# Hybrid backbone step: another order of the mixer's projections, conv's end amid attention, and other halves of the output projection

## Chip, cores and metric

The kernel runs on one core of one Trainium2 chip, in float32 throughout. The metric is device time in microseconds of one execution; lower is better. The kernel before takes 2477.6 us, the median of 3 runs (2476.86 to 2482.67).

## The reference, cut to what matters

Two layers work on 512 latent and 128 context tokens (640 columns in all) of width 1024. Each layer is a half-step FFN, a mixer, and a second half-step FFN. The change touches the mixer alone:

```python
h = _rms(x, norm_g[1]) * (1.0 + sc2) + sh2
u = h @ w_in                                        # 1024 -> 1536 columns
o_pool = _pool_mixer(u[..., :256], pool_w, pool_scale)   # 4 groups: mean over 2/4/8/16 minus token, 64x64 map, scale
glu = u[..., 256:512] * sigmoid(u[..., 512:768])         # conv: value * sigmoid(gate)
y = depthwise_conv(glu, 31 taps, centred) + b
o_conv = silu(_rms(y, conv_norm_g)) @ conv_pw            # 256 -> 256
q, k, v = ...                                       # 8 query heads, 2 key/value heads of 64, RMS norm on q and k
o_attn = context attention, or latent attention (band of +-128 plus 128 cached keys, 2-D rotary), with a sink per head
x = x + g2 * (concat([o_pool, o_conv, o_attn]) @ w_out)  # 256 + 256 + 512 -> 1024
```

## The kernel before, in words

Channels lie on the 128 partitions and tokens along the free axis. Every float32 product is made from three products of a high and a low part (`h*h`, `h*l`, `l*h`), each on 320 of the 640 columns. A chunk of the input projection is 128 output channels: 8 blocks of input channels, 3 parts, 2 halves of the tokens, 48 products in `product`, line 379. `u_chunks` yields two such chunks for a load of 256 columns (1 MB). ScalarE writes the high part of the weights (line 358), VectorE the low part (line 359).

The function is written as generators, and a scheduler puts each engine's instructions in a fixed order from the order in which they are written, a priority, and its own reckoning of time. Engines take their queues in that order and wait on each other by semaphores. `tc.high_priority(offset=AHEAD)` puts an attention batch 200 instructions ahead of where it is written.

`mixer` goes through these pieces. `ORDER` ahead of attention: conv's gate `cg`, keys and values `kv`, the first two query chunks `q0`, conv's value `ca`. Keys take three steps (`k_steps`): their norm, their transposes and caches, and the rotary embedding with the split into high and low part. Queries pass through `query_heads`: square, norm (a chain of small VectorE operations on 128x10), rotary multiplications on POOL, and the split. `BEHIND`, woven into attention: the other query chunks `q1`, pooling `pl` (two chunks and two small products `po`), and the first half of the output projection (`out_chunks`, eight chunks of 24 products).

Attention has four channel pairs `c` of two heads, and each has two batches of blocks, (0, 1) and (2, 3, 4); after a batch there are two or three steps, 20 in all, numbered `i`. A batch makes scores (line 1080, two PSUM banks), takes the maximum on VectorE (line 1083), the exponential and a scaling on ScalarE (1091, 1095), transposes through one bank on TensorE (1098) with copies back on ScalarE (1099), the value products (1105, one bank), and the split into `mixa` (826, 827). At step `i` the loop pops `FILL[i]` modulation steps for later sub-layers, runs taps, conv's steps and `PLAN[i]` background steps.

Conv's 31 taps per channel chunk are `conv_taps`. Chunk 0's taps, and the first and the last four of chunk 1, run on VectorE (lines 928 and 930). The other 26 of chunk 1 are a scaled copy on ScalarE (933) into one scratch buffer `cm` and an addition on POOL (934). `TAP_PLAN` gives the taps of each step. At `i == CONV_AT`, 15 here, the rest of the taps is written and `convolution` begins; it has six steps, one at each `i` from there: sum of squares, norm (323 to 329), its spread (335, 336), a swish of each chunk (1035 to 1044), and two product chunks `cp` with their splits. The last step comes after the loop.

The second half of the output projection is `into_ffn`, line 743: it works half the tokens after the other and goes over into the second FFN. Before, part 0 takes blocks 0, 1, 4, 5 of the concatenated input (pool, and attention's first two pairs), part 1 takes 6, 7, 2, 3 (attention's last two, then conv).

Scratch buffers of 640 or more columns come from one pool of seven (`tmp`), larger ones from one of six (`act`), weights as loaded from one of two (`raw`). The mixer's scaled input `xa` lies in the phase's own pool until its end.

Of the kernel before, what the change touches and what calls it, by code (L numbers as in the profile page):

```python
# [16 lines left out]
P = 128  # L17
D = 1024
KD = D // P
# [32 lines left out]
CONV_AT = 15  # L52
TAP_PLAN = ((3, 2, 1, 2, 3, 2, 0, 2, 2, 1, 3, 2, 0, 2, 1, 3, 1, 1, 1, 3), (2, 4, 3, 3, 4, 4, 4, 2, 0, 4, 1, 1, 0, 1, 2, 1, 2, 0, 1, 4))
ORDER, BEHIND = ("cg", "kv", "q0", "ca"), ("q1", "pl")
PLAN = (0, 1, 0, 1, 0, 2, 0, 1, 0, 0, 0, 1, 1, 1, 2, 1, 1, 1, 1, 0)
# [43 lines left out]
def backbone(ctx: ExitStack, tc: tile.TileContext, ins, consts, y_prompt, y_sample, out_k, out_v):  # L99
# [8 lines left out]
    def phase(name):  # L108

        if "cm" in scope:  # L110
            scope.pop("cm").__exit__(None, None, None)
        cm = tc.tile_pool(name=name, bufs=1, reuse_waits="tile")
        scope["cm"], scope["pool"] = cm, cm.__enter__()

# [268 lines left out]
    def new_xa(name):  # L383
        return tuple(scope["pool"].tile([P, KD, T + 2], F32R, tag="xa", name=f"{name}_{t}", bufs=2) for t in "hl")
# [399 lines left out]
    def mixer(l, xa, R, tab, fill):  # L784
# [179 lines left out]
        def pooling():  # L964
# [39 lines left out]
            catch_up()  # L1004
            for c, (ph, pl) in enumerate(parts):
                w = (pw[0][:, c:c + 1, :], pw[1][:, c:c + 1, :])
                pa, pb = product(w, lambda k: (ph, pl), 1, 0, f"po{l}{c}")
                m = act([P, 2, T], F32R, f"mixp{l}{c}")
# [6 lines left out]


        def convolution():
# [9 lines left out]
            RC = rstd_spread(dg, tmp(f"RC{l}"), bank_pair(f"rc{l}"))  # L1027
# [3 lines left out]
            for c in range(2):  # L1031
# [7 lines left out]
                th = tmp(f"cth{l}{c}")  # L1039
                A.activation(out=th, in_=z, func=AF.Tanh, scale=hg)  # L1040
                V.scalar_tensor_tensor(out=z, in0=th, scalar=1.0, in1=z, op0=ALU.add, op1=ALU.mult)
                hh, hl = tmp(f"ch{l}{c}", dt=F32R), tmp(f"cl{l}{c}", dt=F32R)
# [4 lines left out]
            for c in range(2):  # L1047
                w = split_w(cw_raw, 2, c, f"cpw{l}{c}")
                pa, pb = product(w, lambda k: hs[k], 2, 0, f"cp{l}{c}")
                mh, ml = tmp(f"mch{l}{c}", dt=F32R), tmp(f"mcl{l}{c}", dt=F32R)  # L1050
# [90 lines left out]
        for nm in ORDER:  # L1141
            for _ in pieces[nm]():
                if k_steps and nm != "kv":
                    next(k_steps[0], None)
        catch_up()
# [4 lines left out]
        def background():  # L1150
            for nm in BEHIND:
                yield from pieces[nm]()
            yield from out_chunks([0, 1, 4, 5], 0, lambda m: None)
# [3 lines left out]
        for c in range(4):  # L1157
            m = act([P, 2, T], F32R, f"mixa{l}{c}")
            mix[4 + c] = (m[:, 0, :], m[:, 1, :])
            for blks in BATCHES:  # L1160
                with tc.high_priority(offset=AHEAD):
                    behind = batch(c, blks, m)
                for _ in blks:
# [4 lines left out]
                    for cc in range(2):  # L1168
                        conv_taps(cc, TAP_PLAN[cc][i], behind[cc])
# [9 lines left out]
        for _ in conv:  # L1179
            next(bg, None)  # L1180
# [7 lines left out]
        def load(mp):  # L1188
            raw = wpool.tile([P, 4, 256], F32, tag="raw", name=f"wout{l}_1_{mp}", padded_shape=[P, KD, 256], bufs=BUFS["raw"])
            for i, k in ((0, 6), (2, 2)):  # L1190
# [3 lines left out]
        return into_ffn(l, 2, ins["ffn2_wi"][l], f"p{l}_1", load, lambda k: mix[(6, 7, 2, 3)[k]], gate_of(l, 1, 1.0))  # L1194
# [42 lines left out]
    for l in range(DEPTH):  # L1237
# [4 lines left out]
        def after1(m, l=l, st=st):  # L1242
            if m == 0:
                phase(f"mix{l}")
                st["a"], st["xa"], st["acc"] = prepare(l, 1, f"xa{l}1")
# [73 lines left out]
```

## Time and profile before

| what | value |
|---|---|
| median of 3 runs | 2477.6 us |
| the profiled execution | 2478.26 us |
| its span | 2476.5 us |
| TensorE busy | 2348.3 us (95%) |
| VectorE, ScalarE, POOL busy | 1707.3, 1021.5, 475.7 us (69%, 41%, 19%) |
| mean granted TensorE clock | 0.967 |

The span is the time between the first and the last instruction of the profile; about 1.8 us lie around it. A busy TensorE isn't TensorE at its peak, as its products are pipelined, and a share of the span is an average over stages. In layer 0 the mixer's first product starts at 516.8 us and the second FFN's half of the output projection ends at 808.4; in layer 1 these are 1724.9 and 2020.1.

### The profile page before, as it was taken

Reading aid. Unit: us, or ns where it says so; the run is one execution under the profiler, and the core shown is the slowest. Engines: PE = TensorE matmul, PEld = TensorE weight load, DVE = VectorE, ACT = ScalarE, POOL = GpSimd, SP = SyncE. Lnnn points to the kernel's source line nnn. Section 1 sums busy time; section 2 is a strip of 40 time slices with the busy share of each in tenths; the row PEclk is TensorE's granted clock in tenths of the full one; section 3 lists DMA queues with packets and bytes.
Section 4 is the critical chain, followed back from the end, with each engine's and each line's share of the span. In section 5 each row is a group of like instructions: output and inputs, shape, how many; then the busy total and the mean of one; then the engine's idle time right before and its main releaser. Section 6 shows DMA issues by size and latency. Waiting matters only on the chain.

```text
span 2476.5 us, 40450 instructions
## 1 busy us (share of the span) xinstructions
PE 2348.3 (95%) x16491; PEld 2222.1 (90%) x16491; DVE 1707.3 (69%) x3174; ACT 1021.5 (41%) x1865; POOL 475.7 (19%) x376
## 2 busy tenths in 40 slices
PE   4999999999888899999989999999988889999999
PEld 4899999998568899999989999999975789999998
DVE  4667676667875876676669484858588569585855
ACT  2433333344674533333345242425266545242423
POOL 2101020121431211111132020212024323020210
PEclk7999999999998999999999999999998899999999
DMA  5444332222512123342312424223243022222222
GB/s 172 131 141 132 98 125 69 92 94 91 181 63 71 49 94 128 104 133 94 121 61 82 141 82 141 86 86 101 73 148 134 22 77 69 86 82 81 86 77 77
DMA packets 193990, 246.04 MB, mean 99 GB/s; under 512 B 5705, under 2 KB 176494, under 8 KB 193804
## 3 DMA queue, kind: packets, MB, share of 16 engines
q1 hardware_dynamic: 191824, 240.81, 29.9%
q8 instruction: 130, 2.13, 0.4%
q0 software_dynamic: 512, 1.95, 0.3%
q10 hardware_dynamic: 1468, 0.70, 0.1%
q14 instruction: 56, 0.46, 0.1%
HBM read 240.55 MB, written 2.88 MB: 98 GB/s over the span
## 4 chain that ended last, share of the span: by engine, by line
PE 82%; DVE 10%; ACT 4%; DMA 2%; issue 2%; SPq 0%; POOL 0%; ACTq 0%; DVEq 0%; POOLq 0%
PE f_B L555 11%; PE o_a L379 11%; PE f_C L555 11%; PE o_b L379 11%; PE f_A L555 11%; PE f_D L555 6%; PE f L596 3%; PE p L743 2%; PE mod L266 2%; PE o L743 1%; PE u_q_b L379 1%; PE u_q_a L379 1%; DVE cy L930 1%; DVE xa_l L397 1%; DVE X L421 1%
## 5 line engine op out<-in xcount | busy, mean ns | idle before, releaser
L379 PE MATMUL o_a<-f_h,o_wh 128*128 128x320 f32 x1344 | 402.9, 310 | 0.0
L379 PE MATMUL o_b<-f_h,o_wh 128*128 128x320 f32 x1344 | 401.4, 309 | 0.0
L421 DVE SCALAR_TENSOR_TENSOR X<-o_a,gate,X 128x320 f32<-128x320 f32 x120 | 65.8, 549 | 305.3 <-PE o_a L379 305.0
L379 PEld LDWEIGHTS o_a<-f_h,o_wh 128*128 128x128 f32 x1344 | 251.0, 188 | 8.7 <-ACT o_wh L358 5.8
L547 POOL TENSOR_TENSOR f_t<-f 128x512 f32<-128x512 f32 x80 | 127.6, 1595 | 660.1 <-DMA f<-in_ffn_wi_dram 556.0
L379 PEld LDWEIGHTS o_b<-f_h,o_wh 128*128 128x128 f32 x1344 | 251.4, 188 | 2.9 <-issue 2.9
L358 ACT ACTIVATE o_wh<-wo 128x768 fp32r<-128x768 f32 (+1 forms) x120 | 95.9, 800 | 381.0 <-PE o_b L379 259.7
L654 POOL TENSOR_TENSOR f_t<-f_t,f 128x512 f32<-128x512 f32 x80 | 114.4, 1430 | 638.1 <-DVE f_q_wl L533 332.8
L379 PE MATMUL o_b<-f_h,o_wl 128*128 128x320 f32 x672 | 207.3, 308 | 0.0
L379 PE MATMUL o_a<-f_h,o_wl 128*128 128x320 f32 x672 | 207.0, 308 | 0.0
L531 ACT ACTIVATE f_q_wh<-f_t 128x512 fp32r<-128x512 f32 x140 | 85.9, 629 | 199.5 <-DVE f_t L545 55.0
L379 PEld LDWEIGHTS o_b<-f_h,o_wl 128*128 128x128 f32 x672 | 126.2, 188 | 0.0
L379 PEld LDWEIGHTS o_a<-f_h,o_wl 128*128 128x128 f32 x672 | 126.0, 188 | 0.0
L359 DVE TENSOR_TENSOR o_wl<-wo,o_wh 128x768 fp32r<-128x768 f32 (+1 forms) x120 | 108.2, 903 | 15.6 <-ACT o_wh L358 15.0
L934 POOL TENSOR_TENSOR cy<-cy,cm 128x655 f32<-128x655 f32 x52 | 88.7, 1705 | 148.4 <-ACT cm L933 148.4
L531 ACT ACTIVATE f_P_wh<-f 128x512 fp32r<-128x512 f32 x112 | 66.5, 626 | 120.2 <-PE f_A L555 78.2
L555 PE MATMUL f_B<-F_h,f_q_wl 128*128 128x320 f32 x352 | 108.7, 309 | 0.8 <-DVE f_q_wl L533 0.8
L555 PE MATMUL f_B<-F_h,f_q_wh 128*128 128x320 f32 x352 | 108.7, 309 | 0.2 <-ACT f_q_wh L531 0.2
L555 PE MATMUL f_B<-F_l,f_q_wh 128*128 128x320 f32 x352 | 108.6, 308 | 0.0
L555 PE MATMUL f_C<-F_h,f_m_wh 128*128 128x320 f32 x336 | 103.6, 308 | 0.0
L555 PE MATMUL f_C<-F_l,f_m_wh 128*128 128x320 f32 x336 | 103.6, 308 | 0.0
L555 PE MATMUL f_C<-F_h,f_m_wl 128*128 128x320 f32 x336 | 103.5, 308 | 0.0
(541 smaller groups left out, 7349.9 us busy)
## 6 DMA issues: line engine op xcount, KB each, us to landing
f<-in_ffn_wi_dram SPq DMA_DIRECT2D x88, 1024.0 KB, 5.2
mw<-in_mod_w_dram SPq DMA_DIRECT2D x72, 1024.0 KB, 5.1
wo<-in_ffn_wo_dram SPq DMA_DIRECT2D x48, 768.0 KB, 4.9
wo<-in_ffn_wo_dram SPq DMA_DIRECT2D x16, 512.0 KB, 3.4
wout<-in_w_out_dram SPq DMA_DIRECT2D x32, 256.0 KB, 3.2
win_q<-in_w_in_dram SPq DMA_DIRECT2D x4, 1024.0 KB, 5.1
xt<-in_x_sample_dram SPq DMA_DIRECT2D x4, 512.0 KB, 5.5
win_cg<-in_w_in_dram SPq DMA_DIRECT2D x2, 1024.0 KB, 5.1
```

Of the source, the lines that this page charges most:

```text
L266: PE.matmul(ps[32 * g:32 * g + 32, 0:256], C[:, k, :], w[:, :, g, :], start=(k == 0), stop=(k == KD - 1))
L358: A.activation(out=wh, in_=src, func=AF.Copy)
L359: V.tensor_tensor(out=wl, in0=src, in1=wh.bitcast(F32), op=ALU.subtract)
L379: PE.matmul(ps[:, :n], ww[:, k, :], xx[:, lo:lo + n], start=(k == order[0] and i == 0), stop=(k == order[-1] and i == 2))
L421: V.scalar_tensor_tensor(out=X[:, m, s:e], in0=ps[:, s - o:e - o], scalar=gate[:, m, c:c + 1], in1=X[:, m, s:e], op0=ALU.mult, op1=ALU.add)
L531: A.activation(out=h, in_=src, func=AF.Copy, scale=sign)
L547: G.tensor_tensor(out=t3, in0=self.block(g, 1, 1), in1=self.block(g, 0, 1), op=ALU.add)
L555: PE.matmul(ps[:, :HALF], w[:, kp, :], self.F[f][kp][:, i, :], start=(first and kp == 0 and n == 0), stop=(kp == 3 and n == 2), skip_group ...
L596: PE.matmul(ps[:, :HALF], w[:, k, :], x, start=(k == 0 and n == 0), stop=(k == KD - 1 and n == 2))
L654: G.tensor_tensor(out=t2, in0=t2, in1=self.block(g, 1, 0), op=ALU.add)
L743: PE.matmul(ps[:, :HALF], w[:, m % 2, k, :], x[:, h * HALF:(h + 1) * HALF], start=(k == 0 and n == 0), stop=(k == 3 and n == 2))
L934: G.tensor_tensor(out=y, in0=y, in1=m, op=ALU.add)
```

## The change

The order ahead of attention becomes gate, value, keys, queries. After each of the four chunks of keys and first queries, four taps of both chunks of conv are run; after that two per step, and at step 7 the rest, with `convolution` from there on, so that it ends within the loop. Background steps are spread otherwise. The output projection's part 0 takes pool and conv (blocks 0 to 3), part 1 attention (4 to 7). `xa` moves into a pool of its own, `upper`. Once pooling's chunks have read it, that pool is closed and a new one is opened in its place: two tiles `mixp`, which came from `act`, and ten tiles `part` for conv's end, which came from `tmp`.

```diff
-CONV_AT = 15
-TAP_PLAN = ((3, 2, 1, 2, 3, 2, 0, 2, 2, 1, 3, 2, 0, 2, 1, 3, 1, 1, 1, 3), (2, 4, 3, 3, 4, 4, 4, 2, 0, 4, 1, 1, 0, 1, 2, 1, 2, 0, 1, 4))
-ORDER, BEHIND = ("cg", "kv", "q0", "ca"), ("q1", "pl")
-PLAN = (0, 1, 0, 1, 0, 2, 0, 1, 0, 0, 0, 1, 1, 1, 2, 1, 1, 1, 1, 0)
+CONV_AT = 7
+TAP_EARLY = 4
+TAP_PLAN = 2
+ORDER, BEHIND = ("cg", "ca", "kv", "q0"), ("q1", "pl")
+PLAN = (0, 1, 0, 1, 0, 1, 1, 0, 1, 1, 0, 0, 0, 1, 1, 1, 1, 1, 1, 2)
...
     def phase(name):
 
+        upper(None)
...
+    def upper(name):
+
+        if "upper_cm" in scope:
+            scope.pop("upper_cm").__exit__(None, None, None)
+        if name:
+            cm = tc.tile_pool(name=name, bufs=1, reuse_waits="tile")
+            scope["upper_cm"], scope["upper"] = cm, cm.__enter__()
...
-        return tuple(scope["pool"].tile([P, KD, T + 2], F32R, tag="xa", name=f"{name}_{t}", bufs=2) for t in "hl")
+        return tuple(scope["upper"].tile([P, KD, T + 2], F32R, tag="xa", name=f"{name}_{t}", bufs=2) for t in "hl")
...
             catch_up()
+            upper(f"parts{l}")
             for c, (ph, pl) in enumerate(parts):
...
-                m = act([P, 2, T], F32R, f"mixp{l}{c}")
+                m = scope["upper"].tile([P, 2, T], F32R, tag="mixp", name=f"mixp{l}{c}", bufs=2)
...
+        def part(name, dt=F32R):
+            return scope["upper"].tile([P, T], dt, tag="part", name=name, bufs=10)
...
-            RC = rstd_spread(dg, tmp(f"RC{l}"), bank_pair(f"rc{l}"))
+            RC = rstd_spread(dg, part(f"RC{l}", F32), bank_pair(f"rc{l}"))
...
-                th = tmp(f"cth{l}{c}")
+                th = part(f"cth{l}{c}", F32)
...
-                hh, hl = tmp(f"ch{l}{c}", dt=F32R), tmp(f"cl{l}{c}", dt=F32R)
+                hh, hl = part(f"ch{l}{c}"), part(f"cl{l}{c}")
...
-                mh, ml = tmp(f"mch{l}{c}", dt=F32R), tmp(f"mcl{l}{c}", dt=F32R)
+                mh, ml = part(f"mch{l}{c}"), part(f"mcl{l}{c}")
...
                 if k_steps and nm != "kv":
                     next(k_steps[0], None)
+                if nm in ("kv", "q0"):
+                    for cc in range(2):
+                        conv_taps(cc, TAP_EARLY)
...
-            yield from out_chunks([0, 1, 4, 5], 0, lambda m: None)
+            yield from out_chunks([0, 1, 2, 3], 0, lambda m: None)
...
-                        conv_taps(cc, TAP_PLAN[cc][i], behind[cc])
+                        conv_taps(cc, TAP_PLAN, behind[cc])
...
-        for _ in conv:
-            next(bg, None)
+        assert next(conv, None) is None
...
-            for i, k in ((0, 6), (2, 2)):
+            for i, k in ((0, 4), (2, 6)):
...
-        return into_ffn(l, 2, ins["ffn2_wi"][l], f"p{l}_1", load, lambda k: mix[(6, 7, 2, 3)[k]], gate_of(l, 1, 1.0))
+        return into_ffn(l, 2, ins["ffn2_wi"][l], f"p{l}_1", load, lambda k: mix[4 + k], gate_of(l, 1, 1.0))
...
                 phase(f"mix{l}")
+                upper(f"xa{l}")
```

## Rows read from the trace of the kernel before

**Rows 1.** The page, part 1: busy time, share, instructions.

```profile
PE 2348.3 (95%) x16491; PEld 2222.1 (90%) x16491; DVE 1707.3 (69%) x3174; ACT 1021.5 (41%) x1865; POOL 475.7 (19%) x376
```

**Rows 2.** Windows: stretch, length, busy by engine, clock, DMA share, GB/s.

```profile
553.00:596.00 43.00, 42.55 (x301) 38.88 (x299) 30.62 (x75) 15.98 (x30) 8.40 (x12) 1.00 0.30 104
596.00:741.00 145.00, 125.92 (x920) 95.02 (x920) 118.66 (x273) 97.61 (x210) 54.37 (x40) 0.94 0.33 112
741.00:764.00 23.00, 15.00 (x95) 11.44 (x95) 8.93 (x27) 11.79 (x26) 6.42 (x5) 0.66 0.07 24
764.40:780.40 16.00, 15.27 (x92) 13.79 (x91) 11.79 (x23) 7.71 (x15) 0.00 (x0) 0.96 0.25 78
1806.00:1952.00 146.00, 128.79 (x915) 97.39 (x915) 118.59 (x270) 97.73 (x209) 54.93 (x40) 0.89 0.33 111
1952.00:1976.00 24.00, 16.75 (x97) 12.57 (x96) 8.94 (x27) 12.36 (x28) 6.42 (x5) 0.60 0.07 23
```

**Rows 3.** Waits of TensorE, 596 to 780: us in total, times, longest.

```profile
PE a_0t L1098 <- ACT a_0S L1099: 6.8, 4, 2.1
...
PE a_2s L1080 <- DVE a_2mx L1083: 4.0, 3, 2.4
```

**Rows 4.** Windows, whole core, a stretch of FFN products alone.

```profile
1225.00:1250.00 25.00, 25.00 (x172) 25.00 (x172) 17.66 (x31) 11.08 (x21) 0.67 (x1) 1.00 0.42 132
```

**Rows 5.** Timeline ahead of attention: start, length, engine, line, operation, shapes.

```profile
590.38 0.74 ACT L886 ACTIVATE KS<-KS 64x640 fp32r<-64x640 f32 x1 [0.20 <-DVE KS L885]
...
591.09 2.04 DVE L910 SCALAR_TENSOR_TENSOR glu<-u_ca_t,u_ca_b,u_cg_t 128x512 f32<-128x512 f32 x2
...
595.71 0.56 DVE L1083 CUSTOM_DVE_ANT_0 a_0S<-a_0s,tab 128x384 f32<-128x384 f32 x1
```

**Rows 6.** Groups of layer 0's mixer, conv's taps: busy, mean ns, idle before.

```profile
L934 POOL TENSOR_TENSOR cy<-cy,cm 128x655 f32<-128x655 f32 x26 | 44.7, 1718 | 75.3 <-ACT cm L933 75.3
...
L930 DVE SCALAR_TENSOR_TENSOR cy<-glu,taps,cy 128x655 f32<-128x655 f32 x34 | 34.5, 1014 | 0.7 <-POOL cy L934 0.2
...
L933 ACT ACTIVATE cm<-glu,taps 128x655 f32<-128x655 f32 x26 | 21.7, 835 | 3.9 <-POOL cy L934 3.9
```

**Rows 7.** Windows of line 930 alone: VectorE's ordinary taps.

```profile
596.00:741.00 145.00, 30.86 (x30) 0.94 0.33 112
```

**Rows 8.** Groups of VectorE, 755 to 783: conv's end.

```profile
L1044 DVE SCALAR_TENSOR_TENSOR cl<-cy,chg,ch 128x640 fp32r<-128x640 f32 x2 | 1.8, 881 | 0.1
...
L1035 DVE TENSOR_TENSOR cy<-cy,RC 128x512 f32<-128x512 f32 (+1 forms) x4 | 1.7, 486 | 1.5 <-ACT RC L336 1.5
...
L1041 DVE SCALAR_TENSOR_TENSOR cy<-cth,cy 128x640 f32<-128x640 f32 x2 | 1.6, 812 | 0.0
...
L827 DVE TENSOR_TENSOR mcl<-cp_a,mch 128x320 fp32r<-128x320 f32 x2 | 1.0, 486 | 0.7 <-PE cp_b L379 0.7
```

**Rows 9.** Groups of ScalarE, 755 to 783.

```profile
L1043 ACT ACTIVATE ch<-cy,chg 128x640 fp32r<-128x640 f32 x2 | 1.6, 816 | 0.0
```

**Rows 10.** Timeline of TensorE at the end of attention.

```profile
757.72 2.15 PE L323 MATMUL rc_ss<-ones,ca 128*128 128x1 f32 x10
...
760.12 3.68 PE L1105 MATMUL a_2o<-a_2S,VS 128*64 128x128 f32 x32 [0.26 <-DVE rc_v L325]
```

**Rows 11.** Windows of line 379 behind attention: TensorE, weight loads, clock, DMA.

```profile
764.40:780.40 16.00, 11.79 (x72) 10.80 (x72) 0.96 0.25 78
```

**Rows 12.** Timeline of ScalarE: second pool tile and last attention tile.

```profile
711.55 0.52 ACT L1011 ACTIVATE mixp<-po_a,vec 128x320 fp32r<-128x320 f32 x1
...
763.88 0.49 ACT L826 ACTIVATE mixa<-a_2o 128x384 fp32r<-128x384 f32 x1 [5.64 <-PE a_2o L1105]
```

**Rows 13.** Timeline: a query's norm beside POOL.

```profile
645.65 1.28 POOL L820 TENSOR_TENSOR u_q_t<-u_q_t,tab 128x512 f32<-128x512 f32 x1
...
645.75 1.20 DVE L312 TENSOR_TENSOR rq_w<-rq_y 128x10 f32<-128x10 f32 x1
...
649.81 0.17 DVE L312 TENSOR_TENSOR rq_w<-rq_y 128x10 f32<-128x10 f32 x1
```

## The prediction

> **What bounds the kernel now.** I read the page first: TensorE is busy 95% of the span [rows 1]. An average like that hides stages, so next came the windows of one mixer. Before attention (553 to 596) TensorE idles 0.45 us in 43 at full clock. In the main stretch of attention (596 to 741) it idles 19.1 us of 145, and in the last attention batch (741 to 764) 8.0 us of 23, at a mean granted clock of 0.66; from 764.4 to 780.4 it idles 0.7 us [rows 2]. Layer 1 repeats this: 17.2 us of 146 and 7.3 us of 24, clocks 0.89 and 0.60 [rows 2]. So what the change can touch is roughly 27 us of idle time per layer, plus slow-clock time. Everything outside the mixers is the same.
>
> Then I asked what ends TensorE's idle time in that stretch: copies by ScalarE between transposes, and VectorE's score reductions that free the two score banks [rows 3]. VectorE is busy 118.7 us of 145 there (82%), ScalarE 97.6 (67%) [rows 2]. Main attention is therefore a chain through in-order VectorE and ScalarE queues that are well filled with other work; the last batch is pure latency (VectorE 8.9 us of 23). A later start of attention costs wall time 1:1, and an emptier VectorE gives some of it back.
>
> **The change part by part**, per layer; the two mixers are alike.
>
> *Order.* Two value chunks of 48 products move from behind the queries to ahead of the keys. At full clock TensorE issues a product every 25/172 = 0.145 us [rows 4], so 96 take 13.9 us. No work is added, but keys and the first queries end 13.9 us later, and their chain then has to run: in before it went on to the last key copy at 590.4 + 0.7, and the first score reduction came at 595.7 [rows 5]. What covered this chain was value; now the next ready work covers it, the two chunks of q1 (also 13.9 us), so TensorE should not stand still, but attention starts later. VectorE spent 2.0 us on gating the first value chunk in just that gap [rows 5]; with the scaling of both chunks I put 3.6 us that leave it, an estimate. The early taps put work back: a tap, once begun, takes 1.0 us, and I allow three of them in the chain's way, 2.7 us. 13.9 - 3.6 + 2.7 = **+13 us**. Bounds: +10 (no tap in the way) and +25 (twelve taps more).
>
> *Taps.* Four taps per channel after each of the four chunks of keys and q0: 16 per channel. Channel 0's run on VectorE (1.014 us), channel 1's on ScalarE (0.835) and POOL (1.718), apart from its first [rows 6]. VectorE has 43 - 30.6 = 12.4 us free from 553 to 596 [rows 2] and gains 13 with the later start, so 17 taps fit there: some 17 us of VectorE, 15 x 0.835 = 12.5 of ScalarE and 15 x 1.718 = 25.8 of POOL leave attention. Channel 1's products share one scratch buffer, so ScalarE waits for POOL before each next one, with the keys' and queries' copies queued behind: 3.9 us over all 26 in before [rows 6], inside the tap allowance above.
>
> *Conv's end amid attention.* Steps start at index 7 instead of 15. New inside attention: on VectorE the four groups of [rows 8], 1.8 + 1.7 + 1.6 and 1.0 twice (the second half of the product is alike), 7.1 us; its norm already ran before 764. On ScalarE 1.6 twice (the tanh is as long as the scaled copy) [rows 9] and about 2.5 for smaller copies, 5.7. On TensorE 24 conv products, 3.5 us. Net load of the main stretch: VectorE about -17 x 30/34 + 7.1 = -8 us (30 of its 34 ordinary taps are in that stretch [rows 7], hence the factor), ScalarE -7, POOL -24, TensorE -13.9 (q1) + 3.5. Conv's norm sums and spread now stand amid TensorE's attention work and use the one bank of the value products; if POOL's sum of squares is late, scores and transposes wait behind them. If VectorE keeps its 82% share, -8 is -10 us of wall time. Bounds: 0 if latency alone sets the pace, -15 if TensorE's lighter queue helps in the same measure. I take **-10**, since the waits [rows 3] name both VectorE and ScalarE, and both get lighter.
>
> *The last batch.* Conv's norm sums (2.15 us at the slow clock) stand between the last transposes and the last value products, which wait another 0.26 us for them [rows 10]. They go, and so do three tap copies of 0.835 in ScalarE's queue [rows 6]. Together 4.9 us; not all is on the chain: **-4.5** (bounds 0 and -6).
>
> *After the last batch.* From 764.4 to 780.4 TensorE did 72 products of this line [rows 11]: two output chunks (48, 7.0 us) and conv's (24, 3.5); besides these the norm's spread and a first part of the next half. The plan leaves two chunks for the last step again, so conv's 3.5 us and about 1 us of spread, an estimate, leave: **-4.5** (bounds 0 and -7).
>
> *Output halves.* As many loads, products and residuals; only which channels pair up. Part 0 needs conv instead of attention's first half. Its price is nothing while conv is done in time; cover gone, it is the first rival. In before part 0 waited for the second pool tile, written from 711.6, 52 us ahead of the last attention tile at 763.9 [rows 12]. In after that tile has a buffer of its own.
>
> *Buffers.* Conv's product and norm tiles leave the shared seven scratch buffers and lie where the mixer's input was, after the pool chunks' last read. The load of conv's last weights is the same 0.25 MB, moved past mod loads, and holds one of two raw buffers while mods stream and may make a mod wait; I put nothing for it, since mods are ordered by the plan, and the bound of rival 3 covers it. On SP's queue the loads of value, keys and queries change places, each still a pair of chunks ahead; nothing. The FFN entry finds four more scratch buffers, an estimate from its short waits: **-1** (bounds 0 and -2).
>
> Sum: 13 - 10 - 4.5 - 4.5 - 1 = -7 us per layer, -14 in all. The profiled execution took 2478.3 (span 2476.5 and 1.8 around it), 0.7 over the median of 2477.6. 2478.3 - 14 = **2464 us**. A higher clock in the tail isn't counted; it belongs to the low end.
>
> **Rivals.** (1) *Conv is late.* Conv's last tile gates part 0. On before's clock the first reduction is at 609 and 11 of channel 1's adds are left; they came 4.6 us apart, busy and waiting ((44.7 + 75.3) / 26 [rows 6]): 51 us, then four taps on VectorE, so near 664. Conv's end took 23 us in the tail (norm sums at 757.7 [rows 10] to its last split near 780.4) and is now interleaved: 690 to 700, some 60 us ahead of the last attention tile (609 + 153). Below about 50 us, chunks no longer fit: if four more are left over, 4 x 24 x 0.145 = 14 us per layer; 2464 + 28 = 2492, slower. For it: the chain of one scratch buffer. Against: before attention ScalarE works 16.0 us of 43 [rows 2] and can feed POOL. (2) *Keys held by POOL.* A 128x10 step of the query norm took 1.20 us beside a POOL multiply of 1.28 us, against 0.17 us alone [rows 13]. The moved POOL adds (15 x 1.7 us) now run beside just those norms. Ten steps held so are 10 us and, with POOL's rope queued behind adds, 12 us per layer: 2464 + 24 = 2488, slower. Against: ordinary taps, also VectorE, average only 1.014 beside POOL, and gaps between adds are long. (3) *The start eats the gain*: attention keeps its 168 us, set by latency: 13 - 0 - 4.5 - 4.5 - 0 = +4 per layer to -3: 2472 to 2486, no change. (4) *Attention follows its load*: 10 - 15 - 6 - 7 - 2 = -20 per layer: 2438.
>
> The Trainium skill speaks to (2): "SBUF — State Buffer", section "Who interferes with whom", says that VectorE and POOL share a port pair which whoever comes first holds for its whole instruction, and that a VectorE operation with two SBUF inputs contends with POOL's reads. By that rule all 15 adds could hold the norms, 15 x 1.7 = 26 us per layer as an estimate, a time near 2516; this trace agrees on the single case of 1.20 us, but not that most operations suffer it.
>
> **Numbers.** Forecast (2452 to 2471) 0.40; rival 4 (under 2452) 0.17; rival 3 0.22; rival 1 0.13; rival 2 0.08. Measurement tells 0.3% (7.4 us) from none. Faster 0.57, same 0.22, slower 0.21. Range 2438 to 2488: from rival 4 up to the price of rival 2, which leaves out rival 1's far part and a little below; the likeliest case's own range is 2452 to 2471.
>
> **What would show it.** Start: first score reduction 10 to 16 us later relative to the mixer's start, with q1 products in the gap and no TensorE idle time. Taps: VectorE near full before attention, at least 14 of channel 1's POOL adds before the first reduction. Attention: from first reduction to last tile 168 us falls to some 153. Tail: no conv instruction behind the last value products, two chunks left. Wrong if conv's last tile comes under 50 us ahead of attention's, if TensorE idles ahead of the first scores, or if attention still takes 168 us.

## The result and the profile after

The changed kernel takes 2508.7 us (median of 4 runs, 2508.5 to 2509.7), the kernel before 2478.4 beside it: ratio 1.012, 95% interval 1.0103 to 1.0138. It is slower by some 30 us. The forecast was 2464, and 2508.7 lies above the range's upper end of 2488. The profiled execution has a span of 2506.8 us against 2476.5.

The sum of the page moves little, TensorE from 2348.3 us [rows 1] to this:

```profile
PE 2354.0 (94%) x16491; PEld 2230.5 (89%) x16491; DVE 1719.5 (69%) x3174; ACT 1023.8 (41%) x1865; POOL 479.5 (19%) x376
```

As many instructions, 5.7 us more TensorE time and 30 us more span: TensorE stands still longer. To see where, I cut one mixer (layer 0) at four events: its first product, the first score reduction, the last split of an attention tile, and the next FFN's first product. Between them lie three stages: start, attention and tail. These are the windows of the kernel before, with its last 23 us of attention as the third row (columns as in [rows 2]):

```profile
516.80:595.70 78.90, 77.03 (x507) 72.40 (x505) 50.24 (x117) 26.20 (x46) 11.72 (x15) 0.96 0.29 97
595.70:764.40 168.70, 141.32 (x1013) 106.69 (x1014) 127.90 (x302) 109.77 (x235) 60.79 (x45) 0.90 0.29 99
741.40:764.40 23.00, 15.12 (x93) 11.66 (x94) 8.93 (x28) 11.76 (x25) 6.42 (x5) 0.66 0.07 24
764.40:844.30 79.90, 70.90 (x444) 67.52 (x442) 57.05 (x120) 40.42 (x79) 17.81 (x21) 0.95 0.19 60
```

The same four of the changed kernel:

```profile
517.70:626.40 108.70, 86.07 (x559) 79.01 (x557) 87.70 (x145) 40.49 (x64) 38.83 (x31) 0.87 0.27 91
626.40:799.80 173.40, 154.10 (x1065) 119.60 (x1066) 111.94 (x300) 106.66 (x236) 35.24 (x29) 0.90 0.28 95
776.80:799.80 23.00, 23.00 (x164) 20.84 (x163) 11.04 (x23) 7.39 (x15) 0.00 (x0) 1.00 0.28 85
799.80:861.40 61.60, 54.74 (x343) 52.92 (x342) 41.61 (x95) 31.03 (x63) 19.27 (x21) 0.92 0.14 46
```

Length less TensorE's busy time is its idle time. **Start**: 78.9 to 108.7 us, +29.8; idle 1.9 to 22.6. **Attention and tail** have to be read together, because output chunks move between them (343 products in the tail instead of 444): 248.6 to 235.0, -13.6; idle 36.4 to 26.2. The last 23 us of attention are now full, at a granted clock of 1.00 instead of 0.66. Sum +16.2 us; in layer 1 it is 331.2 to 345.7, +14.5. Together 30.7, where the spans differ by 30.3. So the whole loss is made before the first score, and the later part gains. Of the start's 29.8 us, 20.7 are idle time; the other 9.0 are 52 more TensorE instructions, 32 of modulation and 20 of the second query chunks, that attention held before. The lower granted clock of the start (0.87 instead of 0.96) is not the loss: an instruction there is 0.154 us of busy time, against 0.152 before.

Who holds TensorE in the start? Its waits, 517.7 to 626.4 (us in total, times, longest; `u_q` is a query chunk, `qst` the sums for a query's norm, `mod` a modulation step):

```profile
PE u_q_b L389 <- DVE u_q_t L426: 9.5, 1, 9.5
PE qst L823 <- ACT qsq L950: 4.9, 1, 4.9
PE mod L276 <- DMA mw<-in_mod_w_dram: 3.8, 1, 3.8
```

A query product stood 9.5 us for a PSUM bank that VectorE hadn't emptied. VectorE was not idle meanwhile. Its timeline ahead of that scaling (L426 at 585.57; start, length):

```profile
575.06 2.60 DVE L369 TENSOR_TENSOR u_q_wl<-win_q,u_q_wh 128x1024 fp32r<-128x1024 f32 x1
577.58 2.22 DVE L940 SCALAR_TENSOR_TENSOR cy<-glu,taps,cy 128x655 f32<-128x655 f32 x1
...
580.65 1.53 DVE L319 TENSOR_SCALAR rk_y<-kv 128x10 int32<-128x10 int32 x1
...
583.24 1.46 DVE L325 SCALAR_TENSOR_TENSOR rk_y<-rk_w,rk_y 128x10 f32<-128x10 f32 x1
...
585.57 0.48 DVE L426 TENSOR_TENSOR u_q_t<-u_q_b,r 128x320 f32<-128x320 f32 x1
```

and POOL's at the same time:

```profile
574.81 1.77 POOL L944 TENSOR_TENSOR cy<-cy,cm 128x655 f32<-128x655 f32 x1 [0.96 <-ACT cm L943]
577.53 1.57 POOL L944 TENSOR_TENSOR cy<-cy,cm 128x655 f32<-128x655 f32 x1 [0.95 <-ACT cm L943]
580.05 2.11 POOL L944 TENSOR_TENSOR cy<-cy,cm 128x655 f32<-128x655 f32 x1 [0.95 <-ACT cm L943]
583.11 1.56 POOL L944 TENSOR_TENSOR cy<-cy,cm 128x655 f32<-128x655 f32 x1 [0.95 <-ACT cm L943]
```

Each of the four long VectorE instructions begins while a POOL addition of conv's chunk 1 runs, and ends after it by about its own length or less: 577.66 after 576.58 (weights), 579.80 after 579.10 (tap), 582.18 after 582.16 and 584.70 after 584.67 (norm steps). Undisturbed, such a step is 0.17 us long [rows 13]; with the early taps of conv's chunk 0 alone (an experiment below) these same two steps took 0.17 us each.

### The profile page after: what moved, and what is told of

It reads as the page before. It is cut to its first block, busy times and chain, and to the rows that moved or that the text cites. A ratio compares the mean times of both kernels' runs of the same rounds, so it can differ in the third digit from the quotient of the medians.

```text
span 2506.8 us, 40468 instructions
## 1 busy us (share of the span) xinstructions
PE 2354.0 (94%) x16491; PEld 2230.5 (89%) x16491; DVE 1719.5 (69%) x3174; ACT 1023.8 (41%) x1865; POOL 479.5 (19%) x376
## 3 DMA queue, kind: packets, MB, share of 16 engines
q8 instruction: 130, 2.13, 0.4%
## 4 chain that ended last, share of the span: by engine, by line
PE 81%; DVE 10%; ACT 3%; issue 2%; DMA 1%; POOL 1%; SPq 0%; ACTq 0%; DVEq 0%; POOLq 0%
PE f_B L565 11%; PE f_C L565 11%; PE o_a L389 11%; PE f_A L565 11%; PE o_b L389 11%; PE f_D L565 6%; PE f L606 4%; PE p L753 2%; PE mod L276 2%; DVE cy L940 1%; DMA mw<-in_mod_w_dram 1%; PE p_b L389 1%; PE p_a L389 1%; PE o L753 1%; DVE xa_l L407 1%
## 5 line engine op out<-in xcount | busy, mean ns | idle before, releaser
L431 DVE SCALAR_TENSOR_TENSOR X<-o_a,gate,X 128x320 f32<-128x320 f32 x120 | 65.8, 549 | 305.3 <-PE o_a L389 304.8
L541 ACT ACTIVATE f_q_wh<-f_t 128x512 fp32r<-128x512 f32 x140 | 85.9, 629 | 199.4 <-DVE f_t L555 53.9
L565 PE MATMUL f_B<-F_l,f_q_wh 128*128 128x320 f32 x352 | 108.7, 309 | 0.0
```

The costliest lines, as they stand in the source:

```text
L431: V.scalar_tensor_tensor(out=X[:, m, s:e], in0=ps[:, s - o:e - o], scalar=gate[:, m, c:c + 1], in1=X[:, m, s:e], op0=ALU.mult, op1=ALU.add)
L541: A.activation(out=h, in_=src, func=AF.Copy, scale=sign)
L565: PE.matmul(ps[:, :HALF], w[:, kp, :], self.F[f][kp][:, i, :], start=(first and kp == 0 and n == 0), stop=(kp == 3 and n == 2), skip_group ...
```

## The experiments

All edits start from the changed kernel, apart from "order only" and "before, conv's end at 13", which start from the one before. Times stand beside the kernel before run with them (2476.6 to 2478.0). This table gives layer 0 of each, in us: to the first score reduction, attention to its last tile, from there to the FFN, their sum, and layer 1's sum. The first two rows are the two kernels themselves. Where the text gives no ratio, the time is that of a single run. The stages are those of the one profiled execution, which is not the median: it took 3.7 us more than the time shown in "order only", 5.8 more in "old halves" and 3.8 less in "the same, chunks first".

| kernel | time | start | attention | tail | sum | layer 1 |
|---|---|---|---|---|---|---|
| before | 2478.4 | 78.9 | 168.7 | 79.9 | 327.5 | 331.2 |
| after | 2508.7 | 108.7 | 173.4 | 61.6 | 343.7 | 345.7 |
| order only | 2490.6 | 91.4 | 165.5 | 79.7 | 336.6 | 338.4 |
| no early taps | 2555.3 | 90.0 | 199.1 | 80.3 | 369.5 | |
| early taps of chunk 0 only | 2555.5 | 91.6 | 194.5 | 81.6 | 367.6 | |
| early taps of chunk 1 only | 2488.8 | 97.3 | 174.0 | 65.8 | 337.0 | 335.3 |
| order of before, no early taps | 2536.0 | 79.1 | 198.0 | 78.3 | 355.4 | 362.0 |
| old halves | 2508.3 | 111.9 | 171.6 | 64.1 | 347.6 | 347.4 |
| chunk 1 only, old halves | 2495.6 | 97.3 | 176.0 | 65.5 | 338.8 | 333.1 |
| chunk 1 only, other tap plan | 2494.2 | 98.0 | 177.5 | 61.1 | 336.6 | 338.6 |
| chunk 0 and scratch additions | 2574.3 | 104.6 | 195.3 | 77.7 | 377.6 | |
| order of before, 16 POOL taps | 2505.2 | 80.1 | 179.6 | 82.2 | 341.9 | 343.3 |
| before, conv's end at 13 | 2479.6 | 78.9 | 173.7 | 76.9 | 329.5 | 327.2 |
| no early taps, 16 POOL taps | 2518.6 | 91.5 | 183.9 | 75.2 | 350.6 | 350.6 |
| chunk 1 early on VectorE | 2478.7 | 97.0 | 168.3 | 71.0 | 336.4 | 325.5 |
| the same, chunks first | 2475.7 | 95.3 | 164.9 | 69.5 | 329.7 | 323.7 |

### The start: order, and the two kinds of early taps

**Order only.** The kernel before with one line changed:

```diff
-ORDER, BEHIND = ("cg", "kv", "q0", "ca"), ("q1", "pl")
+ORDER, BEHIND = ("cg", "ca", "kv", "q0"), ("q1", "pl")
```

> The kernel before with only the order gate, value, keys, queries. In before the first score reduction comes 78.9 us after the mixer's first product, in after 108.7 us. Theory A (the early taps hold up keys and queries): the order alone gives 85 to 92 us here, no long wait of TensorE ahead of the scores, and a time of 2478 to 2498 us. Theory B (the order alone, since value no longer covers the keys' chain): 100 us or more, TensorE idle 10 us or more ahead of the scores, and 2500 us or more.

Measured 2490.6, ratio 1.0063 (1.0048 to 1.0078): theory A. The first reduction came 12.5 us later (layer 1: 10.5); attention and tail, 245.2, gave back 3.4, as 34 fewer TensorE instructions stand in attention (979 instead of 1013), 32 of them modulation. The order alone costs 14 us of the 30. Of the 12.5 us, 5.4 are idle time of TensorE: 7.3 us in the start instead of 1.9. The second query chunks hardly moved ahead: by the trace 31 of their 96 products stand before the first reduction, 26 before the change (46 in the changed kernel). TensorE's longest wait in the start is here the one for modulation weights (3.6 us), which the changed kernel shows too.

**No early taps**, **chunk 0 only** and **chunk 1 only**. These divide the early taps:

```diff
-TAP_EARLY = 4
-TAP_PLAN = 2
+TAP_EARLY = 0
+TAP_PLAN = 4
```

```diff
-                    for cc in range(2):
+                    for cc in (0,):
```

and the same line with `(1,)`.

> The kernel after without early taps; four taps per channel and step instead of two, so that conv still begins at step 7. Theory A: the first score reduction moves from 108.7 us back to under 92 us, and the 9.5 us wait of TensorE for a query chunk's scaling is gone; the time falls under 2500 us unless taps in attention cost as much. Theory B: the first reduction stays over 100 us. Theory C (conv's lateness holds back the output chunks and is the main loss): the time stays at 2500 to 2520 whatever the start does, as conv's product still comes some 50 us ahead of the last attention tile or later.

> The kernel after with early taps of channel chunk 0 alone (VectorE), none on ScalarE and POOL. If VectorE's own time is what delays keys and queries, the first reduction stays near 100 to 108 us. If it is POOL's additions that lengthen VectorE's operations, it falls to 85 to 95 us and VectorE's operations ahead of attention have their usual lengths (a chunk's bias of 512 columns near 0.7 us instead of 1.8). The time is not the point: chunk 1's taps then lie late and conv later.

> The kernel after with early taps of channel chunk 1 alone (ScalarE and POOL, its first on VectorE). If POOL's additions are the cause, the first reduction stays at 100 us or more although VectorE has 16 us less to do; if VectorE's own time is, it falls under 95 us.

Measured 2555.3 (1.0327, interval 1.031 to 1.0345), 2555.5 and 2488.8. Without early taps the start came under 92 us as theory A said, but the time lies above what any of the three theories named; "The middle" below is on that. For the start: VectorE's early taps alone add 0.2 us to the 91.4 of the order, which speaks for POOL's additions; POOL's alone add 5.9, which lies between the two answers named; both together add 17.3. They don't add up. In layer 1 the four starts are 91.4 (order alone), 91.5, 98.9 and 109.7 us. The windows from 35.5 us after the mixer's first product to the first reduction show why; here the order alone:

```profile
553.00:608.90 55.90, 50.28 (x342) 45.00 (x342) 35.39 (x83) 18.30 (x33) 8.81 (x7) 0.88 0.33 115
```

with chunk 0's taps:

```profile
555.20:611.30 56.10, 50.60 (x342) 44.81 (x341) 45.50 (x96) 18.53 (x33) 8.83 (x7) 0.88 0.34 115
```

with chunk 1's:

```profile
550.30:612.10 61.80, 51.00 (x339) 45.68 (x339) 48.23 (x82) 29.48 (x48) 34.16 (x22) 0.86 0.31 103
```

and with both, the changed kernel:

```profile
553.20:626.40 73.20, 52.29 (x348) 46.19 (x346) 63.51 (x96) 29.48 (x48) 35.15 (x22) 0.84 0.27 91
```

VectorE's column is the third. Its 96 instructions take 45.5 us without POOL's 15 additions and 63.5 with them; 83 take 35.4 and 82 take 48.2. VectorE has 20.5 us free with the order alone. The taps use 10 of them, the lengthening 13 to 18. The taps alone fit, the lengthening alone costs some 6 us, and both don't fit: TensorE's idle time goes from 5.5 to 20.9 us.

This could still be the taps' own chain (ScalarE's copy, POOL's addition, the one `cm` buffer). **Chunk 0 and scratch additions** takes the chain away and leaves POOL's work:

```diff
-                    for cc in range(2):
+                    for cc in (0,):
                         conv_taps(cc, TAP_EARLY)
+                    for _ in range(4):
+                        d = scope["pool"].tile([P, COUT], F32, tag="sg", name="dum", padded_shape=[P, TMP], bufs=3)
+                        G.tensor_tensor(out=d, in0=glu[1][:, 0:COUT], in1=glu[1][:, 1:1 + COUT], op=ALU.add)
```

> The kernel with only conv's chunk 0 tapped early, plus 16 POOL additions of the same size at the places of the early taps of chunk 1; they read conv's gated value, write a scratch tile, and nothing waits for their result. Theory (POOL's additions lengthen VectorE's instructions that run beside them): the first score reduction comes 102 to 112 us after the mixer's first product instead of 91.6, the VectorE instructions from 35.5 us after that product to the reduction take some 55 to 64 us instead of 45.5, and TensorE idles 12 to 20 us there. Rival (the early taps of chunk 1 delay the start through their chain, ScalarE's copies and the waits between the engines): nothing waits for these additions, so the reduction stays within 3 us of 91.6. The end of the run isn't the point: the taps of chunk 1 come late here as in the kernel it is made from, so about 2555 to 2585.

The reduction came at 104.6 us (105.0 in layer 1), and the same 96 instructions took 58.9 us, as the theory said:

```profile
552.20:621.30 69.10, 54.52 (x342) 47.29 (x341) 58.87 (x96) 18.52 (x33) 36.89 (x23) 0.80 0.27 93
```

Nothing waits for these additions. The next work in POOL's order, the rotary multiplication, comes long after the last of them and waits for VectorE:

```profile
583.25 1.87 POOL L1164 TENSOR_TENSOR dum<-glu 128x655 f32<-128x655 f32 x1
602.71 1.27 POOL L829 TENSOR_TENSOR qr_sh<-qr_sh,tab 128x512 f32<-128x512 f32 x1 [17.59 <-DVE qr_sh L828]
```

So the 13.4 us are theirs as neighbours. Which instructions grow is read from the groups of VectorE in that window; with chunk 0's taps alone:

```profile
L940 DVE SCALAR_TENSOR_TENSOR cy<-glu,taps,cy 128x655 f32<-128x655 f32 x13 | 11.7, 897 | 0.1
L369 DVE TENSOR_TENSOR u_q_wl<-win_q,u_q_wh 128x1024 fp32r<-128x1024 f32 x4 | 4.9, 1218 | 0.0
...
L819 DVE TENSOR_SCALAR u_kv_t<-u_kv_t,u_kv_b 128x512 f32<-128x512 f32 x2 | 1.0, 482 | 0.0
...
L426 DVE TENSOR_TENSOR u_kv_t<-u_kv_b,r 128x320 f32<-128x320 f32 x2 | 1.0, 481 | 0.0
...
L819 DVE TENSOR_SCALAR u_kv_t<-u_kv_t,u_kv_b 128x128 f32<-128x128 f32 x2 | 0.6, 282 | 0.0
```

and with the scratch additions:

```profile
L940 DVE SCALAR_TENSOR_TENSOR cy<-glu,taps,cy 128x655 f32<-128x655 f32 x13 | 19.4, 1493 | 0.2
L369 DVE TENSOR_TENSOR u_q_wl<-win_q,u_q_wh 128x1024 fp32r<-128x1024 f32 x4 | 7.0, 1761 | 0.0
...
L819 DVE TENSOR_SCALAR u_kv_t<-u_kv_t,u_kv_b 128x512 f32<-128x512 f32 x2 | 3.0, 1496 | 0.0
L819 DVE TENSOR_SCALAR u_kv_t<-u_kv_t,u_kv_b 128x128 f32<-128x128 f32 x2 | 2.6, 1298 | 0.0
...
L426 DVE TENSOR_TENSOR u_kv_t<-u_kv_b,r 128x320 f32<-128x320 f32 x2 | 1.0, 476 | 0.0
```

Taps (+7.7 us), weight parts (+2.1) and the bias additions (+2.0, and as much again in their 128x128 form) grow; scalings that read a product from PSUM do not. In the changed kernel the taps of that window grow as well:

```profile
L940 DVE SCALAR_TENSOR_TENSOR cy<-glu,taps,cy 128x655 f32<-128x655 f32 x12 | 15.9, 1326 | 0.1
```

So contention with POOL is shown as a cause: additions that nothing waits for put the first reduction 13.0 us later, where all early taps together put it 17.3 later. The other 4 us were not taken apart; the real additions are also spread out more and have copies on ScalarE ahead of them.

### The middle: conv's norm in TensorE's order

Without early taps of chunk 1 the time was 2555, far above the order's 2491. **Order of before, no early taps** asks whether the new order has a part in that:

```diff
-ORDER, BEHIND = ("cg", "ca", "kv", "q0"), ("q1", "pl")
+ORDER, BEHIND = ("cg", "kv", "q0", "ca"), ("q1", "pl")
-TAP_EARLY = 4
-TAP_PLAN = 2
+TAP_EARLY = 0
+TAP_PLAN = 4
```

> The kernel after with before's order (value behind the queries), so no early taps, and four taps per channel and step; conv from step 7 and the new halves stay. The start should come back to some 79 us after the mixer's first product. If the late start was the main loss, the time falls to 2495 us or less. If conv's lateness is (theory C), conv's last tile comes some 260 us after the mixer's start, the output chunks begin only then, attention stretches to 190 us or more, and the time is 2525 to 2550 us in spite of the early start.

2536.0, as theory C said: the start is that of before, 79.1, conv's last tile comes at 258.3 us, and attention takes 198. TensorE's longest wait there is for conv's norm sums:

```profile
PE rc_ss L333 <- POOL ca L1037: 18.4, 1, 18.4
```

Its order is fixed, conv's norm sums stand amid attention, and POOL's sum of squares isn't there; scores, transposes and chunks stand behind. Without early taps in the new order the same wait is 23.4 us. With 26 taps on POOL, the early taps of chunk 1 are what makes conv's place in the middle possible; in the changed kernel the wait is 0.8.

**Old halves**, alone and with chunk 1's early taps only, asks whether the gate on conv costs anything:

```diff
-            yield from out_chunks([0, 1, 2, 3], 0, lambda m: None)
+            yield from out_chunks([0, 1, 4, 5], 0, lambda m: None)
...
-            for i, k in ((0, 4), (2, 6)):
+            for i, k in ((0, 6), (2, 2)):
...
-lambda k: mix[4 + k]
+lambda k: mix[(6, 7, 2, 3)[k]]
...
-                mh, ml = part(f"mch{l}{c}"), part(f"mcl{l}{c}")
+                mh, ml = tmp(f"mch{l}{c}", dt=F32R), tmp(f"mcl{l}{c}", dt=F32R)
```

> The kernel after with the output projection's old halves (pool and attention's first two pairs, then attention's last two and conv; conv's product tiles back in the shared scratch buffers). Conv still ends amid attention, but no output chunk waits for it. Theory C: the first output chunk moves from 238 us after the mixer's start to 190 to 210, attention shrinks from 173 to 158 to 167 us, and the time falls to 2480 to 2498 us. If attention's pace is set by its own chain, it stays at 172 us or more and the time at 2503 us or more.

> Both changes for the better put together: early taps of channel chunk 1 alone (ScalarE and POOL), and the old halves. With early taps of chunk 1 alone and the new halves the time was 2488.8 us beside 2476.6 of before. If conv's gate on the output chunks costs what theory C says, 2465 to 2482 us; if it costs nothing, 2486 us or more.

2508.3 (1.0122, 1.0105 to 1.0139) and 2495.6 (1.0073, 1.0058 to 1.0088): no gain. The first output chunk came at 242.4 us after the mixer's first product, against 238.4, although nothing in it needs conv. TensorE's timeline of the changed kernel shows what stands in front of it (`rc_ss` are conv's norm sums, `cp` conv's products, `p` an output chunk):

```profile
727.40 0.83 PE L333 MATMUL rc_ss<-ones,ca 128*128 128x1 f32 x6 [0.83 <-POOL ca L1037]
...
747.50 0.41 PE L389 MATMUL cp_a<-ch,cpw_wh 128*128 128x320 f32 x1
...
755.74 0.31 PE L389 MATMUL cp_b<-ch,cpw_wl 128*128 128x320 f32 x1
...
756.14 0.54 PE L389 MATMUL p_a<-mixp,p_wh 128*128 128x320 f32 x2
```

`CONV_AT` and `PLAN` write the chunks behind conv's products, and TensorE takes them so. So these two runs show that the halves are worth nothing in this order of work; what earlier chunks are worth they don't show, as the chunks hardly moved. "Chunks first" below moves them.

**Other tap plan** (chunk 1's early taps only, and chunk 0's taps four per step):

```diff
-                        conv_taps(cc, TAP_PLAN, behind[cc])
+                        conv_taps(cc, (4, 2)[cc], behind[cc])
```

> Early taps of channel chunk 1 alone, the new halves, and chunk 0's taps at four per step instead of two with a lump of fifteen at step 7. Conv's norm sums then come some 10 us earlier. Theory C: the output chunks begin as much earlier and the time falls from 2488.8 us to 2478 to 2486. If VectorE's taps in early attention matter more than conv's end, it stays or rises.

2494.2 in one run, 5.4 above the single run without this edit. The edit didn't do what it was meant to: conv's norm sums came 2.0 us earlier in layer 0 (201.7 instead of 203.7 us) and 3.4 later in layer 1, not some 10 earlier. So it leaves theory C untested.

**16 POOL taps** shortens POOL's chain otherwise, in the run with the order of before and in the run without early taps:

```diff
-POOL_TAPS = 26
+POOL_TAPS = 16
```

> The changed kernel with the order of before and no early taps, as in the earlier run that took 2536, and with 16 instead of 26 taps of chunk 1 on POOL; the ten others go to VectorE at the end of the chain. Theory (in that run TensorE stood 18.4 us at conv's norm sums in its fixed order, waiting for POOL's sum of squares, with scores and chunks behind it): the wait falls under 3 us, the norm sums come some 30 us earlier, conv ends ahead of the last attention tile, and the tail is as short as in the changed kernel (62 us against 80): 2536 less twice 30 is about 2470, under the 2477 of before. Rival (the ten additional taps stand in VectorE's order and wait for POOL's chain, so the wait only changes its engine): 2510 or more.

> The changed kernel without early taps (2555 in its run) and with 16 instead of 26 taps of chunk 1 on POOL. Theory (as for the order of before): the wait of TensorE at the norm sums, 23.4 us there, falls under 5; the first reduction stays at 90 us; 2555 less twice 32 is about 2490, slower than before by what the later start costs, and 15 to 25 us slower than the same kernel with the order of before. Rival (the lost time in that run has another cause): 2530 or more.

2505.2 (1.0109, 1.0094 to 1.0124) and 2518.6; 2470 and 2490 were expected, so both miss. The wait at the norm sums went (18.4 to none in the list, 23.4 to 8.0), and 31 and 37 us with it. But with the order of before the rest is still a loss of 27 us against before. Its windows, attention and tail:

```profile
597.50:777.00 179.50, 142.92 (x971) 104.68 (x972) 133.72 (x310) 106.10 (x234) 45.78 (x35) 0.84 0.26 90
777.00:859.20 82.20, 75.11 (x487) 73.22 (x486) 54.24 (x121) 36.02 (x71) 19.23 (x21) 0.96 0.19 65
```

TensorE idles 36.6 us in attention, 27.4 before, and 487 products are left for the tail: the first chunk came at 245.5 us, 177.7 before. My theory that the wait was all was wrong there.

**Before, conv's end at 13** takes only the earlier end:

```diff
-POOL_TAPS = 26
-CONV_AT = 15
+POOL_TAPS = 20
+CONV_AT = 13
```

> The kernel before with two numbers changed: conv's end begins at step 13 instead of 15, and 20 instead of 26 taps of chunk 1 are on POOL. Theory (what is worth something in the change is conv's end ahead of the last tile, and it can be had without moving the start): first reduction at 79 us as before, POOL's last addition some 25 us earlier than 233, conv's last tile at about 245 instead of 266, the stretch from the last attention tile to the next FFN's first product 68 to 72 us instead of 80: 2477 less twice 8 to 12 is about 2457. Rival (TensorE meets conv's norm sums too early and waits there, as in the run with the order of before): attention grows by what the tail loses, 2477 or more.

2479.6, ratio 1.0001 (0.9988 to 1.0015); 2457 was expected. The norm sums moved from 240.9 to 231.6 us, conv's last tile from 265.8 to 260.6; the tail lost 3.0 us and attention grew by 5.0 (in layer 1 the tail lost 4.6 and attention grew by 0.7). The time is that of the kernel before: conv's end alone, brought forward with VectorE paying for it, is worth nothing that the runs can tell.

### Without POOL beside the start

**Chunk 1 early on VectorE** is "chunk 1 only" with these sixteen taps on VectorE:

```diff
-                    elif c == 0 or tp > POOL_TAPS:
+                    elif c == 0 or tp < 16 or tp > POOL_TAPS:
```

**Chunks first** adds to it the old halves (as above) and

```diff
-CONV_AT = 7
+CONV_AT = 12
-PLAN = (0, 1, 0, 1, 0, 1, 1, 0, 1, 1, 0, 0, 0, 1, 1, 1, 1, 1, 1, 2)
+PLAN = (0, 1, 0, 1, 0, 2, 0, 1, 0, 0, 0, 1, 1, 1, 2, 1, 1, 1, 1, 0)
```

> The changed kernel with early taps of chunk 1 alone, and these sixteen on VectorE; POOL has 11 taps of chunk 1 left, in attention. Beside it stands the run with the same early taps on POOL: 2488.8, first reduction at 97.3 us, TensorE's idle time from 35.5 us to the reduction 10.8. Theory (POOL's additions are what costs at the start beyond the order): the reduction comes at 91 to 93 us as in the runs with the order alone and with VectorE's early taps, TensorE idles about 5.5 us there, conv's norm sums are no later than 204 us, and the time is 2488.8 less twice 5 to 6, about 2478, that is no change against before: the order's later start eats what conv's earlier end gives. Rival (VectorE with sixteen more taps of its own delays the keys and queries as much as POOL did): reduction at 97 or later, 2489 or more.

> The kernel with sixteen early taps of chunk 1 on VectorE, with the halves and the background plan of before and conv's end from step 12, so that TensorE's order has output chunks ahead of conv's norm and products. Theory A (chunks behind conv leave TensorE without work in the middle of attention): the first output chunk comes at 185 to 195 us instead of 235, attention falls from about 172 to 160 to 165, and the time is 8 to 15 us under that of the run beside it, near 2466, a gain against before. Theory B (TensorE's idle time in attention is that of the chain through VectorE and ScalarE, about 25 us wherever the chunks stand: 27.4 before, 26.2 with the order alone, 25.4 with early POOL taps): the chunks move, the tail has fewer of them, and the time stays within 5 us of the run beside it.

The first: 2478.7, ratio 1.0007 (0.9998 to 1.0016). The time is as expected, 10 us under the same taps on POOL, but the way to it only half: the reduction came at 97.0 and 93.8 us in the two layers (97.3 and 98.9 with POOL), and TensorE idled 8.5 us ahead of it in layer 0, not 5.5. So the start gave 5 us in all and the later part the rest, nearly all of it in layer 1; layer 0's sum hardly moved (336.4 instead of 337.0), and its first reduction stayed at the rival's 97. Sixteen more taps of its own delay VectorE too, in layer 0 as much as POOL's additions did. The 10 us also rest on a single run with the taps on POOL.

The second: 2475.7, ratio 0.9995 (0.9985 to 1.0005). The first chunk moved from 235.7 to 187.3 us, and the time by 3 us, which the two intervals don't separate: theory B by its time. Attention did shrink as theory A said (to 164.9 and 161.2 us), but in layer 1 the tail grew by 9.5. So where the chunks stand decides little here. Attention and tail take 234.4 us, 14.2 less than before (20.3 less in layer 1); the start takes 16.4 more (12.9 in layer 1). That is the balance of the idea without POOL's additions beside the start, and no kernel here is measurably faster than the one before.

## Why the prediction was wrong

**The failed step is *Order*, with the tap allowance in it.** It said +13 us, at most +25, and that "TensorE should not stand still"; the trace has +29.8 (layer 1 +28.8) and 20.7 us more of idle TensorE. Its two parts differ. The order's own part was 13.9 - 3.6 = 10.3, and the run with the order alone has 12.5 and 10.5. The size is right, but in part by luck: the two chunks of q1 were to cover the chain, only 5 more of their products moved ahead, and 5.4 us of the 12.5 are idle time. The taps' part was 2.7 us for "three of them in the chain's way" (three at the 1.0 us given there are 3.0); it is 17.3.

**Why 2.7 became 17.3.** The sum had no term for VectorE operations that grow beside POOL's additions. *Taps* reckoned that 17 taps fit VectorE's free time at 1.014 us each [rows 6]. That number is a mean of a stretch where POOL's additions are 4.6 us apart; in it 30 of the 34 taps took 0.86 to 0.99 us and four 1.63 to 2.13. The taps took 0.90 us each without POOL's additions and 1.49 with packed ones (1.33 in the changed kernel), and they are not alone: the weights' low parts and biases in front of keys and queries grow too, 13 to 18 us of VectorE time. What is late next is the emptying of a query's PSUM bank, the 9.5 us wait above. Rival 2 named this mechanism, with a chance of 0.08 and 12 us, for the norm steps alone; it is what happened, in more kinds of instruction than it named (the two long norm steps above cost 2.7 us together, the twelve taps of that stretch 12 x (1.326 - 0.897) = 5.1). The argument against it in the prediction, that ordinary taps "average only 1.014 beside POOL", read a mean of mostly undisturbed taps as if all were beside POOL.

The Trainium skill, "SBUF — State Buffer", section "Who interferes with whom", states the lock for VectorE operations with two SBUF inputs, and that a `tensor_scalar` can contend too in a two-port mode. Trace and scratch additions agree on both (tap 0.90 to 1.49, bias 0.48 to 1.50) and on PSUM-fed scalings, which stayed at 0.48. The prediction's estimate from it was 26 us per layer, for the norms; 13.4 of 28.1 us of scratch additions came out as VectorE time.

**Conv's end amid attention, last batch, after the last batch, buffers**: -20 in sum. Measured -13.6 for attention and tail. VectorE's busy time in attention fell by 16.0 us, POOL's by 25.6 and ScalarE's by 3.1, where I had -8, -24 and -7 for the main stretch; yet attention did not fall to 153 but grew to 173.4. It held 1065 TensorE instructions instead of 1013, and the tail 101 fewer: 77 products of the output projection and conv's 24 came in, 20 products of q1 (the prediction took all 96 out) and 32 of modulation went to the start. "VectorE keeps its 82% share" was the wrong rule: over all of attention its share fell from 76 to 65%, and TensorE's idle time only from 27.4 to 19.3 us. Of the 13.6 the order gives 3.4 (245.2 with it alone). The last batch came out better than said: TensorE full, at a granted clock of 1.00, no conv instruction behind the last value products.

**Output halves** at 0: right, 2508.3 against 2508.7 with the old ones. The cover was thinner than reckoned: conv's last tile came at 244.0 us, 38 ahead of the last attention tile and not 60. POOL's eleven late additions were paced by ScalarE's copies, which stand in attention's queue (57.6 us of waiting for them from 600 to 720): the last began at 199.4 us after the mixer's start, where the prediction's 609 + 51 us had its end near 660 - 517 = 143. By rival 1's own condition (under 50) chunks should have been left over; none were. The condition was too strict: eight chunks of 24 products at 0.145 us [rows 4] are 27.8 us, which 38 us hold. Rival 1 proper appears in the runs without early taps of chunk 1, where it costs up to 47 us against the changed kernel, not through the gate of the halves but through the norm sums in TensorE's order.

**What would show it**: POOL additions ahead of the first reduction 15 (at least 14): right. VectorE 63.5 of 73.2 us, near full: right, but from lengthening. First reduction 10 to 16 us later and no idle TensorE: wrong. Attention at 153: wrong. Tail: half right. No conv instruction stands behind the last value products, but no chunk of the first half is left either; all eight are done, and the second half's products begin at 795.1, 4.7 us ahead of the last tile.

**Left open**: what keeps some 18 to 37 us of TensorE idle in attention where no long wait at conv's norm sums stands; the waits name copies, reductions and modulation weights by turns, and no run here took that chain apart.

## What to carry to other kernels

Before moving work to an idle engine, ask which engine's instructions will run beside it: a mean duration from one stretch holds only for that stretch's overlap, so price the operation both alone and beside its new neighbour. An in-order engine pays for a late producer with all that stands behind: place a step by when its input is ready (18 to 23 us here), and check what the fixed order puts in front of freed work before giving that work another dependence. When work can move between two stages, add the stages up; attention grew by 4.7 us, and attention and tail together still fell by 13.6.

## What was not expected of the hardware

Beside packed POOL additions a VectorE tap falls into step with them. VectorE's timeline with the scratch additions, and POOL's:

```profile
561.32 0.48 DVE L425 TENSOR_TENSOR u_kv_t<-u_kv_a,r 128x320 f32<-128x320 f32 x1
...
563.15 2.30 DVE L369 TENSOR_TENSOR u_q_wl<-win_q,u_q_wh 128x1024 fp32r<-128x1024 f32 x1
565.37 2.72 DVE L819 TENSOR_SCALAR u_kv_t<-u_kv_t,u_kv_b 128x512 f32<-128x512 f32 x2
...
568.01 7.43 DVE L940 SCALAR_TENSOR_TENSOR cy<-glu,taps,cy 128x655 f32<-128x655 f32 x4
```

```profile
557.06 28.06 POOL L1164 TENSOR_TENSOR dum<-glu 128x655 f32<-128x655 f32 x16 [28.11 <-DVE glu L920]
```

Four taps take 7.43 us, 1.86 each instead of 0.90. POOL goes on at 28.06 / 16 = 1.75 us each, little over its 1.718 [rows 6]; the shortest additions of that size in the kernel before took 1.57. At that rate POOL loses 16 x 0.18 = 2.9 us, an estimate, and VectorE 13.4: VectorE pays most. A bias addition, one large input in two pieces, takes 0.48 + 0.28 us alone and 2.72 here, relatively more than a tap.
